# Decayed queries of each GLA head in a tile padded with zeros, in a hybrid GLA and HGRN2 decoder layer

## The chip, the cores and the metric

The kernel runs on one core of a Trainium2 chip. The metric is the device time of one execution in microseconds (us); smaller is better. Times are medians of several executions. A profile is one execution, recorded instruction by instruction. The engines are named as the profile names them: PE is TensorE (matmuls), PEld its loading of the stationary operand, DVE is VectorE, ACT is ScalarE, POOL is GpSimd, SP the engine that issues most DMAs.

## The reference

One decoder layer over 2048 tokens of width 1024, in float32: a mixer with two kinds of heads side by side (four GLA heads with 64 channels, four HGRN2 heads with 128 channels, all with values of width 128), an output projection, and an MLP with a squared ReLU. What the change touches is the gated linear attention of the heads:

```python
def step(S, inp):
    qi, ki, vi, bi = inp
    ...
    scores = jnp.einsum('bhid,bhjd,bhijd->bhij', qi, ki, decay)
    o = jnp.einsum('bhij,bhjv->bhiv', scores, vi) + jnp.einsum('bhid,bhdv->bhiv', qi * jnp.exp(bi), S)
    b_last = bi[:, :, -1:, :]
    S = S * jnp.exp(b_last)[:, :, 0, :, None] + jnp.einsum('bhjd,bhjv->bhdv', ki * jnp.exp(b_last - bi), vi)
    return S, o
```

Each chunk of tokens makes an output from two products: the masked scores with the values, and the decayed queries with the state carried so far.

## The kernel before

The tokens are worked in four blocks of 512, each of four chunks of 128 (the kernel's chunk is twice the reference's). In each block the mixer goes through four units in the order 0, 2, 3, 1. Units 0 and 1 hold two GLA heads each, units 2 and 3 two HGRN heads each. A unit first projects queries and keys with channels on the partitions (`zchan`), then values and gates with tokens on the partitions (`values`). These projections are the bulk of the work: each is three matmuls of 512 columns with operands split into a high and a low part (L301, L302, L303, "wide" in what follows).

The attention itself is a generator, `tile_task`, that is stepped between pieces of the projections. For a GLA unit the two heads share one tile: head 0 has its 64 channels on partitions 0 to 63, head 1 on 64 to 127. For HGRN a head fills the 128 partitions. The steps are:

- `decays`: cumulative sums of the log decays, three exponentials on ACT, then on DVE the products of keys and decay (L665) and of queries and decay (L666).
- `transposed` and `scores`: the keys are transposed on PE and copied by ACT (L723); the scores are made by L711 and L712, with 64 rows for a GLA head, and DVE writes them under the mask into a tile PT (L714, L715).
- `states`: one product of keys and values for each chunk (L735 for GLA, L738 for HGRN) and on DVE the running state of the four chunks in a tile St: L751 for the first, then L752 (add) and L754 (scale) for each further one. For GLA the two heads' states lie on the two halves of the partitions of one St.
- `outputs`: for each chunk, scores with values (L765) and queries with the state (L766), summed in one bank. L766 takes `q[rows, cols]` and `St[rows, cols]`, where `rows` is one half of the partitions for a GLA head and all 128 for HGRN.
- normalising, gating, a transpose back (L633), and the output projection.

All of this is full float32 (no split), and a product of this kind stands in the trace as two matmuls. The last unit's attention runs beside the output projection. DVE also does the second half of each sigmoid (L319, L547, L476) and the low parts of operands. The order on each engine is set ahead of time: instructions are placed by a scheduler that simulates the program with its own costs, so an edit at one place can move instructions of neighbouring tasks on every engine. Waits between engines are semaphores; each engine works through its own list in order.

`stage` gives [128, 1024] tiles from a pool of three (tag "st"). Before the change, two are only reserved at the start, and the pool is used from the end of the mixer on.

Of the kernel before, what the change touches and what calls it, by code (L numbers as in the profile page):

```python
# [16 lines left out]
P = 128  # L17
# [4 lines left out]
TB = 512  # L22
# [124 lines left out]
class Layer:  # L147
# [234 lines left out]
    def setup_mixer(self):  # L382
        nc = self.nc
        self.load_const("cmask")
        self.normw = self.static("norm_w", [P, 8])
        self.b_gk = self.static("b_gk", [P, 2])
        wgk = self.ct()[:16, :256]
        nc.sync.dma_start(wgk, self.io["w_gk_up"])
        self.wgk = self.split(self.small("wgk", (16, 256), F32R), self.small("wgk", (16, 256), F32R), wgk)
        lbr = self.static("hgrn_lower_bounds", [P, 4, 2])  # L390
        mx, den, self.lb, self.oml = (self.small(x, (P, 4)) for x in ("lbm", "lbd", "lb", "oml"))
        e = self.small("lbe", (P, 4, 2))
        nc.vector.tensor_max(mx, lbr[:, :, 0], lbr[:, :, 1])
        for r in range(2):
            nc.vector.tensor_sub(e[:, :, r], lbr[:, :, r], mx)
        nc.scalar.activation(e, e, AF.Exp)
        nc.vector.tensor_add(den, e[:, :, 0], e[:, :, 1])
        nc.vector.reciprocal(den, den)
        nc.vector.tensor_mul(self.lb, e[:, :, 0], den)
        nc.vector.tensor_scalar(self.oml, self.lb, -1.0, 1.0, ALU.mult, ALU.add)  # L400
        self.S, self.PT, self.npt = [], [], 0
        for i in range(6):
            self.S.append(self.small("S", (P, P)))
            nc.vector.memset(self.S[-1], 0.0)
        for i in range(2 if self.exact else 3):
            self.PT.append(self.small("PT", (P, TB)))
            nc.vector.memset(self.PT[-1], 0.0)
# [190 lines left out]
    def tile_task(self, u, i, q, k, g, scale):  # L598

        gla = u < 2  # L600
        heads = [(0, slice(0, 64)), (1, slice(64, P))] if gla else [(i, slice(0, P))]
        r, pts = yield from self.decays(q, k, g, scale)
        while self.vdone[u] < 3 and not self.exact:
            yield
        v, sg = self.vg[u]
        kT = self.transposed(k)
        if pts is None:
            pts = [self.next_pt() for _ in heads]
            mask = self.c["cmask"].unsqueeze(1).broadcast_to([P, NCH, P])
            for pt, (h, rows) in zip(pts, heads):  # L610
                self.scores(pt, q, k, rows, mask)
        yield
        while self.vdone[u] < 4:
            yield
        yield
        St = self.states(kT, r, v, gla, i, u if gla else 2 + 2 * (u - 2) + i)
        yield
        outs = []
        for pt, (h, rows) in zip(pts, heads):
            outs.append((h, *self.outputs(pt, q, St, v, h, rows)))  # L620
        yield
        for n, (h, o, rs) in enumerate(outs):
            og = self.ct()
            for j in range(NCH):
                cols = slice(j * P, (j + 1) * P)
                self.nc.vector.scalar_tensor_tensor(og[:, cols], o[:, cols], rs[:, j:j + 1],
                                                    sg[:, j, h * P:(h + 1) * P], ALU.mult, ALU.mult)
            outs[n] = (h, og)
        yield
        for h, og in outs:  # L630
            tr = self.at()
            for j in range(NCH):
                self.nc.tensor.transpose(tr[:, j * P:(j + 1) * P], og[:, j * P:(j + 1) * P], self.c["ident"])  # L633
            n = 2 * u + h
            self.oT[n] = self.split(*self.aslots(), tr, self.normw[:, n:n + 1])

    def decays(self, q, k, g, scale):

        nc, c = self.nc, self.c
        b = self.ct()  # L640
# [5 lines left out]
        r = self.t([P, 2, NCH], "r", bufs=6)  # L646
        if not self.exact:
            mid = b3[:, :, 63]
            d = g.rearrange("p (c t) -> p c t", t=P)
            nc.vector.tensor_sub(d, b3, b3[:, :, 63:64].broadcast_to([P, NCH, P]))  # L650
            nc.vector.tensor_scalar(g, g, LIMIT / scale, -LIMIT / scale, ALU.min, ALU.max)
            f = self.t([P, NCH], "fl", bufs=4)
            nc.vector.tensor_sub(r[:, 0, :], last, mid)
            flag = c["flag_a"] if scale != 1.0 else c["flag_b"]
            nc.vector.tensor_sub(f, b3[:, :, 0], mid)
            nc.vector.tensor_max(flag, flag, f)
            nc.vector.tensor_scalar_mul(f, r[:, 0, :], -1.0)
            nc.vector.tensor_max(flag, flag, f)
            nc.vector.tensor_copy(r[:, 1, :], mid)
            yield  # L660
            nc.scalar.activation(b, g, AF.Exp, scale=-scale)
            nc.scalar.activation(g, g, AF.Exp, scale=scale)
            nc.scalar.activation(r, r, AF.Exp, scale=scale)
            yield
            nc.vector.tensor_mul(k, k, b)  # L665
            nc.vector.tensor_mul(q, q, g)  # L666
            yield
            return r, None
        heads = (slice(0, 64), slice(64, P)) if scale != 1.0 else (slice(0, P),)
        pts = [self.next_pt() for _ in heads]  # L670
        for l, h in enumerate(LEVELS):
            mask = self.t([P, TB], "cti", I32, bufs=1)
# [22 lines left out]
        nc.scalar.activation(b, b, AF.Exp, scale=scale)  # L695
        nc.vector.tensor_mul(q, q, b)
        yield
        return r, pts

    def next_pt(self):  # L700
        self.npt += 1
# [851 lines left out]
```

## Time and profile before

| | |
|---|---|
| median of the timed runs | 2272.21 us (three runs, 2270.02 to 2276.08) |
| the profiled execution | 2269.14 us, span from first to last instruction 2267.3 us |
| granted TensorE clock | 0.995 |
| instructions in the span | 30672 |
| HBM read and written | 289.44 MB and 136.45 MB, 188 GB/s |

The mixer takes the first 960 us of the span; the MLP follows. In the profile a group of instructions has its line, engine, operation, output and input names, shape and count, then busy time in us and the mean of one in ns, then the idle time of the engine before it and what ended that. A timeline row has the start in us, the length drawn, engine, line, operation, names, shape and count. Matmuls are pipelined: the length drawn of one reaches over the start of the next, so the distance from start to start says what a matmul takes of the engine.

### The profile page before, as it was taken

How to read it: one execution, taken by the hardware profiler on the slowest of the kernel's cores; microseconds unless marked ns; L12 is line 12 of the kernel's file. 1: busy time of each engine (PE TensorE's matmuls, PEld its weight loads, DVE VectorE, ACT ScalarE, POOL GpSimd, SP SyncE). 2: the span in 40 equal slices, each digit the busy share in tenths (PEclk: the TensorE clock that was granted, in tenths of full speed). 3: DMA queues.
4: the chain of work that ended last, by engine and by line, in shares of the span. 5: the costliest groups of instructions: out<-in, count | busy, mean ns of one | idle time of the engine just before them, and what ended most of it. 6: DMA issues, size and time to landing. Idle time of an engine off the chain costs nothing.

```text
span 2267.3 us, 30672 instructions
## 1 busy us (share of the span) xinstructions
PE 2216.5 (98%) x10922; PEld 1830.8 (81%) x10922; DVE 1408.5 (62%) x2264; ACT 1089.3 (48%) x2104; POOL 643.5 (28%) x444
## 2 busy tenths in 40 slices
PE   8999999999999999999999999999999999999996
PEld 7788888888888978876888888888778878888884
DVE  6764565343652575377765686656536876777687
ACT  6764565334543554365555565555643322333255
POOL 4444301010100220035522343322322332232344
PEclk9999999999999999999999999999999999999998
DMA  7766974467545974378844474443434433443356
GB/s 244 262 232 241 322 257 149 138 237 281 181 151 176 349 286 158 130 270 281 294 151 152 177 238 163 152 153 144 176 126 135 130 123 110 130 140 117 116 148 132
DMA packets 249810, 428.02 MB, mean 189 GB/s; under 512 B 19872, under 2 KB 93872, under 8 KB 249648
## 3 DMA queue, kind: packets, MB, share of 16 engines
q1 hardware_dynamic: 245520, 418.10, 53.6%
q0 software_dynamic: 3552, 6.82, 1.9%
q8 instruction: 88, 1.44, 0.3%
q10 hardware_dynamic: 576, 1.05, 0.1%
q14 instruction: 74, 0.61, 0.1%
HBM read 289.44 MB, written 136.45 MB: 188 GB/s over the span
## 4 chain that ended last, share of the span: by engine, by line
PE 48%; DVE 2%; DMA 2%; ACT 2%; issue 1%; POOL 1%; SPq 0%; DVEq 0%; ACTq 0%; POOLq 0%
PE Y_f L1057 3%; PE Y_f L1059 3%; PE Y_f L1058 3%; PE Y_f L1358 3%; PE Y_f L1359 3%; PE Y_f L1360 3%; PE X_f L1358 2%; PE X_f L1360 2%; PE X_f L1359 2%; PE Z_f L1059 2%; PE Z_f L1057 2%; PE Z_f L1058 2%; PE Z_f L1360 2%; PE Z_f L1359 2%; PE Z_f L1358 2%; PE X_f L1059 2%
## 5 line engine op out<-in xcount | busy, mean ns | idle before, releaser
L301 PE MATMUL zp_f<-w_f,act_f 128*128 128x512 f32 (+2 forms) x896 | 328.6, 367 | 4.2 <-DVE ct_f L319 3.3
L302 PE MATMUL zp_f<-w_f,act_f 128*128 128x512 f32 (+2 forms) x896 | 325.0, 363 | 0.0
L303 PE MATMUL zp_f<-w_f,act_f 128*128 128x512 f32 (+2 forms) x896 | 323.4, 363 | 0.0
L944 ACT ACTIVATE u_f<-raw_f 128x1024 fp32r<-128x1024 f32 x107 | 113.6, 1061 | 331.9 <-PE Y_f L1359 225.4
L310 POOL TENSOR_TENSOR rs_f<-ms_f,c_neghalf 128x1 f32<-128x1 f32 (+1 forms) x80 | 65.1, 820 | 658.0 <-DVE ms_f L308 657.5
L938 POOL TENSOR_TENSOR u_f<-raw_f,u_f 128x1024 fp32r<-128x1024 f32 x49 | 120.4, 2457 | 305.5 <-ACT u_f L944 304.5
L301 PEld LDWEIGHTS zp_f<-w_f,act_f 128*128 128x128 f32 x896 | 168.6, 188 | 31.3 <-DVE ct_f L319 3.7
L303 PEld LDWEIGHTS zp_f<-w_f,act_f 128*128 128x128 f32 x896 | 168.7, 188 | 25.3 <-issue 0.5
L302 PEld LDWEIGHTS zp_f<-w_f,act_f 128*128 128x128 f32 x896 | 168.9, 189 | 24.3 <-issue 0.5
L301 PE MATMUL zp_f<-act_f,w_f 128*128 128x512 f32 x384 | 151.9, 399 | 7.9 <-ACT act_f L294 7.9
L302 PE MATMUL zp_f<-act_f,w_f 128*128 128x512 f32 x384 | 152.3, 397 | 0.1
L303 PE MATMUL zp_f<-act_f,w_f 128*128 128x512 f32 x384 | 151.9, 395 | 0.0
L1313 DVE TENSOR_TENSOR acc_f<-acc_f,Y_f 128x1024 f32<-128x1024 f32 (+1 forms) x91 | 107.5, 1182 | 64.5 <-PE Y_f L1360 63.2
L1358 PE MATMUL Y_f<-act_f,u_f 128*128 128x512 f32 x368 | 142.3, 390 | 4.8 <-ACT Y_f L1350 2.6
L1359 PE MATMUL Y_f<-act_f,u_f 128*128 128x512 f32 x368 | 143.4, 390 | 0.0
L1360 PE MATMUL Y_f<-act_f,u_f 128*128 128x512 f32 x368 | 142.8, 390 | 0.0
L292 POOL TENSOR_TENSOR w_f<-wr_f,w_f 128x512 fp32r<-128x512 f32 (+1 forms) x76 | 105.3, 1395 | 106.1 <-ACT w_f L291 105.4
L944 ACT ACTIVATE w_f<-t_f 128x512 fp32r<-128x512 f32 x128 | 80.1, 629 | 109.7 <-PE Y_f L1058 56.6
L1059 PE MATMUL X_f<-act_f,w_f 128*128 128x512 f32 x256 | 100.2, 391 | 3.6 <-DVE w_f L941 2.7
L1077 DVE TENSOR_TENSOR ev_f<-Y_f,p_f 128x512 f32<-128x512 f32 x94 | 64.6, 688 | 62.8 <-PE Y_f L1059 62.7
L1313 DVE TENSOR_TENSOR acc_f<-acc_f,Z_f 128x1024 f32<-128x1024 f32 (+1 forms) x62 | 73.2, 1181 | 47.6 <-PE Z_f L1360 47.4
L941 DVE TENSOR_TENSOR w_f<-t_f,w_f 128x512 fp32r<-128x512 f32 x96 | 79.9, 832 | 36.7 <-ACT w_f L944 36.7
(294 smaller groups left out, 5767.0 us busy)
## 6 DMA issues: line engine op xcount, KB each, us to landing
w_f<-w_split SPq DMA_DIRECT2D x188, 512.0 KB, 6.3
raw_f<-u_operands SPq DMA_DIRECT2D x224, 256.0 KB, 3.0
u_operands<-ev_f SPq DMA_DIRECT2D x223, 256.0 KB, 2.1
w_split<-w_f SPq DMA_DIRECT2D x64, 512.0 KB, 5.2
wr_f<-in_w_up SPq DMA_DIRECT2D x62, 512.0 KB, 3.5
wide_f<-in_x SPq DMA_DIRECT2D x32, 512.0 KB, 6.9
wr_f<-in_w_mix SPq DMA_DIRECT2D x64, 256.0 KB, 5.0
wr_f<-in_w_down SPq DMA_DIRECT2D x28, 512.0 KB, 4.8
```

The costliest lines, as they stand in the source:

```text
L301: mm(out, a[0], b[0], start=i == 0, stop=False)
L302: mm(out, a[0], b[1], start=False, stop=False)
L303: mm(out, a[1], b[0], start=False, stop=i == n - 1)
L938: nc.gpsimd.tensor_tensor(out, a, b, op)
L944: self.nc.scalar.activation(hi, raw, AF.Copy)
L1057: mm(z, whi[:, k, :], hi, start=first and k == 0, stop=False, skip_group_check=more)
L1058: mm(z, whi[:, k, :], lo, start=False, stop=False, skip_group_check=more)
L1059: mm(z, wlo[:, k, :], hi, start=False, stop=end, skip_group_check=more)
L1313: nc.vector.tensor_add(a[:, cols], a[:, cols], z[:, cols])
L1358: mm(zx, hi[:, k, tok], whi, start=not loaded and k == 0, stop=False, skip_group_check=loaded)
L1359: mm(zx, hi[:, k, tok], wlo, start=False, stop=False, skip_group_check=loaded)
L1360: mm(zx, lo[:, k, tok], whi, start=False, stop=k == 1, skip_group_check=loaded)
```

## The change

The decayed queries of a GLA tile are no longer written over the queries. A tile `self.queries` of [128, 1024] is made once and zeroed: its first 512 columns belong to head 0 of the unit, its last 512 to head 1. `decays` writes head 0's 64 rows of the product into the first half and head 1's 64 rows into the second; the rows of the other head's channels stay zero. `scores` still takes 64 rows, now from these tiles. `outputs` takes all 128 rows of a head's tile and of St, so that the other head's state is multiplied by zeros. The tile is shared by both GLA units and all blocks. HGRN heads and the exact variant (which is built but not run on this data) compute what they did.

```diff
@@ setup_mixer
+        if not self.exact:
+            x = self.stage()
+            nc.vector.memset(x, 0.0)
+            self.queries = [x[:, :TB], x[:, TB:]]
@@ tile_task
-        r, pts = yield from self.decays(q, k, g, scale)
+        r, pts, qs = yield from self.decays(q, k, g, scale)
...
-            for pt, (h, rows) in zip(pts, heads):
-                self.scores(pt, q, k, rows, mask)
+            for pt, qh, (h, rows) in zip(pts, qs, heads):
+                self.scores(pt, qh, k, rows, mask)
...
-        for pt, (h, rows) in zip(pts, heads):
-            outs.append((h, *self.outputs(pt, q, St, v, h, rows)))
+        for pt, qh, (h, rows) in zip(pts, qs, heads):
+            outs.append((h, *self.outputs(pt, qh, St, v, h, rows if self.exact else slice(0, P))))
@@ decays
             nc.vector.tensor_mul(k, k, b)
-            nc.vector.tensor_mul(q, q, g)
-            yield
-            return r, None
+            qs = self.queries if scale != 1.0 else [q]
+            for qh, rows in zip(qs, (slice(0, 64), slice(64, P)) if scale != 1.0 else (slice(0, P),)):
+                nc.vector.tensor_mul(qh[rows], q[rows], g[rows])
+            yield
+            return r, None, qs
```

Lines move by up to seven: L666 becomes L673, L754 becomes L761, L765 and L766 become L772 and L773. The order on SP stays the same, as does that of every engine after the mixer; PE, DVE, ACT and POOL change places within the mixer, mostly near the tiles of unit 0.

On VectorE, in the last block's unit 0, the product of queries and decay stands so before (ct_f are the [128, 512] working tiles; L476, L579, L596 belong to HGRN heads of unit 2):

```order
L643 SCALAR_TENSOR_TENSOR ct_f_7920<-c_ones,ct_f_7796 128x128 x4
L666 TENSOR_TENSOR ct_f_7238<-ct_f_7238,ct_f_7790 128x512
L596 TENSOR_TENSOR c_fmin<-c_fmin,fm_f_7894 128x1
L579 TENSOR_SCALAR ct_f_7797<-ct_f_7797 128x512
L476 TENSOR_TENSOR ct_f_7865<-zp_f_7803,ct_f_7865 128x512
L650 TENSOR_TENSOR ct_f_7796<-ct_f_7920 128x512
```

And so now (st_f_250 is the tile of padded queries):

```order
L648 SCALAR_TENSOR_TENSOR ct_f_7929<-c_ones,ct_f_7804 128x128 x4
L673 TENSOR_TENSOR st_f_250<-ct_f_7246,ct_f_7798 64x512
L600 TENSOR_TENSOR c_fmin<-c_fmin,fm_f_7902 128x1
L583 TENSOR_SCALAR ct_f_7805<-ct_f_7805 128x512
L673 TENSOR_TENSOR st_f_250<-ct_f_7246,ct_f_7798 64x512
L480 TENSOR_TENSOR ct_f_7873<-zp_f_7811,ct_f_7873 128x512
```

One instruction of 128 rows has become two of 64, with two HGRN steps between them.

A little later on VectorE, in the same tile, the state's updates (L752 and L754 on ct_f_8048) stand so among the HGRN steps before:

```order
L754 TENSOR_SCALAR ct_f_8048<-ct_f_8048,r_f_7855 128x128
L319 SCALAR_TENSOR_TENSOR ct_f_8011<-zp_f_7942,ct_f_8011 128x512
L651 TENSOR_SCALAR ct_f_7935<-ct_f_7935 128x512
L656 TENSOR_TENSOR c_flag_b<-c_flag_b,fl_f_8132 128x4
L752 TENSOR_TENSOR ct_f_8048<-ct_f_8048,at_f_8039 128x128
L657 TENSOR_SCALAR fl_f_8132<-r_f_8129 128x4
L754 TENSOR_SCALAR ct_f_8048<-ct_f_8048,r_f_7855 128x128
L658 TENSOR_TENSOR c_flag_b<-c_flag_b,fl_f_8132 128x4
L476 TENSOR_TENSOR ct_f_8011<-zp_f_7942,ct_f_8011 128x512
L752 TENSOR_TENSOR ct_f_8048<-ct_f_8048,at_f_8039 128x128
L665 TENSOR_TENSOR ct_f_7936<-ct_f_7936,ct_f_8124 128x512
L754 TENSOR_SCALAR ct_f_8048<-ct_f_8048,r_f_7855 128x128
```

And so now, from behind the first of the three scalings (L759 and L761 on ct_f_8057):

```order
L656 TENSOR_SCALAR ct_f_7944<-ct_f_7944 128x512
L319 SCALAR_TENSOR_TENSOR ct_f_8020<-zp_f_7951,ct_f_8020 128x512
L661 TENSOR_TENSOR c_flag_b<-c_flag_b,fl_f_8141 128x4
L759 TENSOR_TENSOR ct_f_8057<-ct_f_8057,at_f_8048 128x128
L662 TENSOR_SCALAR fl_f_8141<-r_f_8138 128x4
L670 TENSOR_TENSOR ct_f_7945<-ct_f_7945,ct_f_8133 128x512
L761 TENSOR_SCALAR ct_f_8057<-ct_f_8057,r_f_7863 128x128
L663 TENSOR_TENSOR c_flag_b<-c_flag_b,fl_f_8141 128x4
L480 TENSOR_TENSOR ct_f_8020<-zp_f_7951,ct_f_8020 128x512
L759 TENSOR_TENSOR ct_f_8057<-ct_f_8057,at_f_8048 128x128
L673 TENSOR_TENSOR ct_f_8020<-ct_f_8020,ct_f_7944 128x512
L761 TENSOR_SCALAR ct_f_8057<-ct_f_8057,r_f_7863 128x128
```

The key product of an HGRN head (L665, now L670) has moved ahead of the second scaling, and a query product of an HGRN head (L666, now L673), which stood behind the third scaling before, now stands ahead of it.

On TensorE, between the second and the third state products of that tile, before (at_f are output banks, zp_f_8139 a bank of a projection):

```order
L301 MATMUL zp_f_8139<-w_f_7729,act_f_7092 128x512
L302 MATMUL zp_f_8139<-w_f_7729,act_f_7092 128x512
L303 MATMUL zp_f_8139<-w_f_7729,act_f_7092 128x512
L766 MATMUL at_f_8086<-ct_f_8048,ct_f_7238 128x128
L765 MATMUL at_f_8086<-wide_f_7353,PT_f_264 128x128
L766 MATMUL at_f_8105<-ct_f_8048,ct_f_7238 128x128
L765 MATMUL at_f_8105<-wide_f_7353,PT_f_266 128x128
```

And now:

```order
L301 MATMUL zp_f_8148<-w_f_7737,act_f_7100 128x512
L302 MATMUL zp_f_8148<-w_f_7737,act_f_7100 128x512
L303 MATMUL zp_f_8148<-w_f_7737,act_f_7100 128x512
L301 MATMUL zp_f_8148<-w_f_7739,act_f_7121 128x512
L302 MATMUL zp_f_8148<-w_f_7739,act_f_7121 128x512
L303 MATMUL zp_f_8148<-w_f_7739,act_f_7121 128x512
L301 MATMUL zp_f_8148<-w_f_7741,act_f_7140 128x512
L302 MATMUL zp_f_8148<-w_f_7741,act_f_7140 128x512
L303 MATMUL zp_f_8148<-w_f_7741,act_f_7140 128x512
L301 MATMUL zp_f_8148<-w_f_7775,act_f_7161 128x512
L773 MATMUL at_f_8095<-ct_f_8057,st_f_250 128x128
L772 MATMUL at_f_8095<-wide_f_7361,PT_f_266 128x128
```

The third state product now has ten wide matmuls ahead of it where there were three.

More of the change, by code (lines that the diff above doesn't have):

```diff
@@ L697, in decays @@
         yield
-        return r, pts
+        return r, pts, [q] * len(heads)
     def next_pt(self):
```

## The prediction

> **What bounds the kernel now.** First I read the busy time of each engine on the page, then the same for the mixer alone (80 to 960 us, where all the changed work lies), then the list of waits of TensorE.
>
> ```profile
> PE 2216.5 (98%) x10922; PEld 1830.8 (81%) x10922; DVE 1408.5 (62%) x2264; ACT 1089.3 (48%) x2104; POOL 643.5 (28%) x444
> 80.00:960.00 880.00, 879.95 (x4988) 733.27 (x4988) 463.28 (x1200) 431.95 (x1088) 145.54 (x135) 1.00 0.63 220
> PE zp_f L301 <- ACT act_f L294: 7.9, 1, 7.9
> PE zp_f L301 <- DVE ct_f L319: 3.3, 1, 3.3
> ```
>
> In the second row the columns are the stretch, its length and the busy time of PE, PEld, DVE, ACT and POOL. PE is busy for 879.95 of 880 us, at a granted clock of 1.00. Of the waits the longest, 7.9 us, is the start, and the second row leaves 0.05 us for all that fall into its stretch. So in the mixer TensorE is the bound, and what counts there is how far apart its matmuls start, not how long each is drawn. VectorE is at 463 of 880 us, but it is not spread evenly, and that decides a part below.
>
> **The change, part by part.** *The state products.* The groups of L766, told apart by shape, show the 64-row ones (GLA) and the 128-row ones (HGRN) of the same line. Each product in full float32 stands as two matmuls ("pieces") in the trace, so 128 pieces are 64 products.
>
> ```profile
> L766 PE MATMUL at_f<-ct_f,ct_f 64*128 64x128 f32 x128 | 27.2, 323 | 0.0
> L766 PE MATMUL at_f<-ct_f,ct_f 128*128 128x128 f32 x128 | 22.4, 275 | 0.0
> ```
>
> By duration alone the two differ little (27.2 against 22.4 us). The start times say more. This is PE's timeline in the outputs of the last GLA tile (start, length drawn, line, shape, number):
>
> ```profile
> 952.25 0.39 PE L302 MATMUL zp_f<-w_f,act_f 128*128 128x512 f32 x1
> 952.57 0.49 PE L766 MATMUL at_f<-ct_f,ct_f 64*128 64x128 f32 x2
> 952.98 0.49 PE L765 MATMUL at_f<-wide_f,PT_f 128*128 128x128 f32 x2
> 953.40 0.49 PE L766 MATMUL at_f<-ct_f,ct_f 64*128 64x128 f32 x2
> 953.82 0.49 PE L765 MATMUL at_f<-wide_f,PT_f 128*128 128x128 f32 x2
> 954.24 0.49 PE L766 MATMUL at_f<-ct_f,ct_f 64*128 64x128 f32 x4
> 954.66 0.49 PE L765 MATMUL at_f<-wide_f,PT_f 128*128 128x128 f32 x2
> 955.08 0.48 PE L766 MATMUL at_f<-ct_f,ct_f 64*128 64x128 f32 x2
> 955.49 0.49 PE L765 MATMUL at_f<-wide_f,PT_f 128*128 128x128 f32 x2
> 955.91 0.49 PE L766 MATMUL at_f<-ct_f,ct_f 64*128 64x128 f32 x2
> 956.32 0.50 PE L303 MATMUL zp_f<-w_f,act_f 128*128 128x512 f32 x1
> 956.66 0.39 PE L301 MATMUL zp_f<-w_f,act_f 128*128 128x512 f32 x1
> ```
>
> And this is the same code for an HGRN head, where both lines have 128 rows:
>
> ```profile
> 122.90 0.39 PE L301 MATMUL zp_f<-act_f,w_f 128*128 128x512 f32 x1
> 123.13 0.38 PE L765 MATMUL at_f<-wide_f,PT_f 128*128 128x128 f32 x2
> 123.35 0.39 PE L766 MATMUL at_f<-ct_f,ct_f 128*128 128x128 f32 x2
> 123.58 0.39 PE L765 MATMUL at_f<-wide_f,PT_f 128*128 128x128 f32 x2
> 123.80 0.39 PE L766 MATMUL at_f<-ct_f,ct_f 128*128 128x128 f32 x2
> 124.02 0.39 PE L765 MATMUL at_f<-wide_f,PT_f 128*128 128x128 f32 x2
> 124.17 0.48 PE L302 MATMUL zp_f<-act_f,w_f 128*128 128x512 f32 x1
> 124.48 0.39 PE L303 MATMUL zp_f<-act_f,w_f 128*128 128x512 f32 x1
> ```
>
> A wide matmul (L301 to L303, 512 columns) takes 0.23 us from start to start (122.90 to 123.13). The HGRN stretch, 122.90 to 124.48, holds two wide ones and five products: (1.58 - 0.46) / 5 = 0.224 us for a product. The GLA stretch, 952.25 to 956.66, holds two wide ones and ten products (six of L766, four of L765): (4.41 - 0.46) / 10 = 0.395 us. The L765 between them are slow too (0.42 us from 952.98 to 953.40), though their shape is that of HGRN: it is the going over between 64 and 128 rows that costs, on both sides of each group of 64-row pieces. With 128 rows the ten would take 2.24 us, so this stretch gives 1.71 us for its six products, 0.285 each.
>
> A tile of unit 0 is laid out a little differently. Its outputs in the last block, first L765 to the wide one behind the last L766:
>
> ```profile
> 820.52:829.87 9.35, 9.35 (x48) 6.56 (x47) 9.29 (x26) 4.29 (x10) 2.62 (x2) 1.00 0.62 240
> 87.55 0.49 PE L766 MATMUL at_f<-ct_f,ct_f 64*128 64x128 f32 x2
> ```
>
> Two of the 48 began before; of the other 46, 14 are wide and 32 are the pieces of 8 L765 and 8 L766. (9.35 - 14 x 0.23) / 16 = 0.383 us; at 0.224 the 16 take 3.58 instead of 6.13 us: 2.55 us for the tile, 0.32 for each L766. From 87.55 to 955.91 us I count 56 such groups of 64-row pieces, seven in each of eight tiles. So the four tiles of unit 0 give 4 x 2.55 = 10.2 us, the four of unit 1 give 4 x (1.71 + 2 x 0.32) = 9.4 us: 19.6 us in all. After the change none of the 56 is left; the scores (L711, L712) and L735 keep their small shapes and their price.
>
> One rule speaks against this. On "TensorE: Matmul & The Clock Gate", section "Part 3: Packing small matmuls — row/col tiling", the Trainium skill says that matmuls on different row groups of the array run beside each other, some 4 ns apart. By it two 64-row products of two heads cost what one does, and zeros throw that away; by the rows above only the x4 at 954.24 has it (0.42 us for two products), one group in seven, and I keep the 19.6 us.
>
> *What VectorE gets more.* The product of queries and decay becomes two of 64 partitions by 512.
>
> ```profile
> L666 DVE TENSOR_TENSOR ct_f<-ct_f,ct_f 128x512 f32<-128x512 f32 x24 | 17.0, 707 | 1.1 <-ACT ct_f L662 1.1
> L714 DVE COPY_PREDICATED PT_f<-c_cmask,at_f 64x512 f32<-64x512 int32 x32 | 23.3, 727 | 37.6 <-PE at_f L712 37.6
> L407 DVE MEMSET PT_f<- 128x512 f32 x3 | 1.5, 485 | 0.2
> ```
>
> No row shows a 64x512 product. It lies between half of 707 ns (nothing is added) and 707 ns (one whole product is added); I take the upper end, since the nearest row with 64 partitions of 512 (L714, 727 ns) is no shorter than one with 128: 0.7 us in each of eight tiles, 5.6 us in all. It lies beside the wide matmuls of a busy PE and costs nothing where VectorE has time to spare; without that cover it is the 5.6 us. The zeroing (128x1024, about 2 x 0.485 = 1 us) lies at the start, where TensorE waits 7.9 us for an ACT result anyway: 0, or 1 us if that cover were gone. The tile is the third of its pool; its next taker comes after the mixer, and a whole unit lies between two uses of it, so new waits for its release cost 0.
>
> *What is late next.* In the unit-0 tile of the last block VectorE is busy for 9.29 of 9.35 us. There the state that L766 reads is ready only just in time. L754 writes it:
>
> ```profile
> 823.35 0.34 DVE L754 TENSOR_SCALAR ct_f<-ct_f,r_f 128x128 f32<-128x128 f32 x1
> 824.12 0.48 PE L766 MATMUL at_f<-ct_f,ct_f 64*128 64x128 f32 x2
> 825.90 0.34 DVE L754 TENSOR_SCALAR ct_f<-ct_f,r_f 128x128 f32<-128x128 f32 x1
> 826.49 0.48 PE L766 MATMUL at_f<-ct_f,ct_f 64*128 64x128 f32 x2
> 828.72 0.33 DVE L754 TENSOR_SCALAR ct_f<-ct_f,r_f 128x128 f32<-128x128 f32 x1
> 829.11 0.49 PE L766 MATMUL at_f<-ct_f,ct_f 64*128 64x128 f32 x4
> ```
>
> The three have 0.43, 0.25 and 0.06 us to spare. Take the last: TensorE would be there 6 x 0.32 = 1.9 us sooner by the six products before it; the new order puts seven more wide matmuls before it (1.6 us later); VectorE reaches L754 0.7 us later by the added product and another 0.7 us later because the new order puts one HGRN product more before it. 0.06 - 1.9 + 1.6 - 1.4 = -1.6 us: TensorE waits 1.6 us of this tile's 2.55. Behind the waiting L766 stand only matmuls, which lose the same. The first tile is nearly as crowded (third figure of engine time in this row, VectorE, 18.88 of 20 us):
>
> ```profile
> 80.00:100.00 20.00, 19.95 (x131) 14.91 (x130) 18.88 (x52) 12.84 (x29) 2.83 (x3) 1.00 0.75 259
> ```
>
> I charge it with 0.5 us, nearer to nothing than to the 1.6 of the last block, since its state products have more wide matmuls between them. Together 2.1 us; bounds are 0 and the whole 10.2 us of the unit-0 tiles.
>
> **Sum.** 19.6 - 2.1 = 17.5 us less. The rows come from an execution of 2269.14 us (span 2267.3), which becomes 2251.6. That execution lies 3.07 us under the median of the timed runs, 2272.21 (2270.02 to 2276.08), so the forecast for the median is 2254.7 us, 0.77% faster. After 960 us the order of instructions is the same on every engine; the stage behind moves up as it is.
>
> **The rivals.** (1) *VectorE becomes the bound* in all four unit-0 tiles, not in one: their 10.2 us go, and the added product, 4 x 0.7 = 2.8 us, shows. Gain 19.6 - 10.2 - 2.8 = 6.6 us, 2265.6 us. For it: 9.29 of 9.35 us. Against it: in the sum above even the most crowded tile keeps a third of its gain. (2) *Only durations count*: the slow starts beside the 64-row pieces have another reason (the order, the full-float32 L765), and 27.2 - 22.4 = 4.8 us is all: 2267.4 us. Against it: HGRN runs the same two lines in the same alternation at 0.224. (3) *Lost overlap, the slower side*: zeros double the rows that are run for nothing. If the two heads' 64-row products had all run beside each other, 64 products cost 32 x 0.224 = 7.2 us before and 64 x 0.224 = 14.3 us now: 7.2 us more, 2279.4 us (+0.3%). It decides only if such pairs are the rule and the going over is free; the rows show one pair in seven groups. That the change does not do what it says is not open: all 64 products have 128 rows in the new order.
>
> **How the numbers follow.** The forecast has 0.84, with a range of its own from 2250 to 2261; (1) has 0.08, (2) 0.04, (3) 0.04. The low end, 2249, takes 64 x 0.32 = 20.5 us, no new wait, and the lowest of the runs shown (2.2 us under their median). The high end, 2264, takes half the unit-0 gain away (19.6 - 2.1 - 5.1 = 12.4 us) and the scatter upward (3.9 us); it leaves out (1), (2) and (3), 0.16. A measurement of this kernel can tell about 0.3% from no change, 6.8 us. So faster holds the forecast, 0.84; within 0.3% are (1) and (2), 0.12; slower is (3), 0.04.
>
> **What would show it.** Right, if the line that was L766 has one shape, 128*128, if ten products of a GLA stretch take about 2.2 us and the L765 between them 0.22 us each, and if TensorE now has waits of about 1.6 us in all for the state update (L754) near 810 us. The product of queries should stand as 64x512 at 0.7 us, twice in each tile. Wrong, if the L765 beside the state products stay at 0.42 us (2), if waits for VectorE add up to 10 us in the four unit-0 tiles (1), or if TensorE gains what I say and a new wait after 960 us takes it back.

## The result and the profile after

The changed kernel takes 2256.22 us, the median of six runs (2252.61 to 2258.14); the kernel before took 2272.32 us beside it (2269.99 to 2276.08, six runs). The ratio is 0.9929, with a 95% interval of 0.9919 to 0.9939: 16.1 us faster, with an interval of 13.9 to 18.4 us. The forecast was 2254.7 us, in a range from 2249 to 2264.

The profiled execution of the changed kernel took 2258.14 us (span 2256.3), the longest of its six, and that of before 2269.14 us, shorter than any of the six runs above. So the two traces differ by 11.0 us and the medians by 16.1; the runs of the two kernels once more, below, show where this difference lies.

Lines from 600 on have moved down by up to seven: L766 is now L773, L765 is L772, L754 is L761, L666 is L673, L715 is L722. First the busy times of the page, then the groups of PE between 80 and 945 us, told apart by shape, that answer to those of before:

```profile
PE 2201.9 (98%) x10922; PEld 1830.0 (81%) x10922; DVE 1416.8 (63%) x2273; ACT 1090.1 (48%) x2104; POOL 643.5 (29%) x444
```

```profile
L772 PE MATMUL at_f<-wide_f,PT_f 128*128 128x128 f32 x256 | 46.7, 275 | 1.2 <-DVE PT_f L722 1.2
L773 PE MATMUL at_f<-ct_f,st_f 128*128 128x128 f32 x128 | 24.0, 279 | 2.5 <-DVE ct_f L761 2.5
L773 PE MATMUL at_f<-ct_f,ct_f 128*128 128x128 f32 x128 | 22.5, 275 | 0.4 <-DVE ct_f L761 0.4
```

The products with the state have one shape; those of GLA are the ones that read `st_f`, the padded tiles. Behind the second bar stands idle time of PE before them, which was 0.0 for the state products of before: 2.9 us for the state update L761 (2.5 of them before GLA products, 0.4 before an HGRN product), 1.2 us for the masked scores L722. PE's timeline in the outputs of the last GLA tile, the place that the prediction shows of before:

```profile
940.09 0.39 PE L302 MATMUL zp_f<-w_f,act_f 128*128 128x512 f32 x1
940.32 0.38 PE L773 MATMUL at_f<-ct_f,st_f 128*128 128x128 f32 x2
940.54 0.39 PE L772 MATMUL at_f<-wide_f,PT_f 128*128 128x128 f32 x2
940.76 0.39 PE L773 MATMUL at_f<-ct_f,st_f 128*128 128x128 f32 x2
...
942.10 0.39 PE L772 MATMUL at_f<-wide_f,PT_f 128*128 128x128 f32 x2
942.32 0.39 PE L773 MATMUL at_f<-ct_f,st_f 128*128 128x128 f32 x2
942.47 0.48 PE L303 MATMUL zp_f<-w_f,act_f 128*128 128x512 f32 x1
942.78 0.40 PE L301 MATMUL zp_f<-w_f,act_f 128*128 128x512 f32 x1
```

From 940.09 to 942.78 it is 2.69 us where it was 4.41; less two wide matmuls (0.46) the ten products take 0.223 us each, as HGRN's did. The L772 beside them start 0.22 us apart, not 0.42, with no change to them.

To follow the time through the program, take the same wide matmul (by its place in PE's list) in two traces and compare its start. L303 behind this tile stood at 956.32 us before and stands at 942.47 now: 13.85 us earlier. The table does this by stretches of the mixer, bounded by wide matmuls that start at 80.5, 230.1, 812.3, 906.9 and 994.1 us in the first trace of before. Each number is what the stretch gained against that trace, in us; the last two columns are the sum at the end of the mixer (here the last L303, at 994.1 us before, behind the output projection) and at the last wide matmul of the program. The other rows are the experiments that follow.

| kernel | start | block 1: both GLA tiles | blocks 2, 3: four tiles | block 4: unit 0 | block 4: unit 1 | mixer | program |
|---|---|---|---|---|---|---|---|
| changed | -0.7 | 3.1 | 9.7 | -0.5 | 2.3 | 13.9 | 10.9 |
| changed, once more | -0.3 | 2.9 | 9.5 | -0.5 | 2.3 | 13.8 | 9.7 |
| before, once more | 0.0 | 0.0 | -0.4 | -1.0 | 0.0 | -1.4 | -4.5 |
| e1, split only | 0.0 | -1.3 | -0.4 | -2.6 | 0.0 | -4.3 | -6.4 |
| e2, rows only | -0.4 | 4.3 | 9.7 | -0.2 | 2.3 | 15.7 | 13.4 |
| e3, pairs | 0.1 | 3.3 | 5.6 | 0.3 | 1.3 | 10.6 | 8.5 |
| e4, scores of 128 rows | -0.2 | 3.4 | 8.2 | -1.2 | 2.0 | 12.1 | 8.5 |
| e5, half product on GpSimd | -1.4 | 4.0 | 9.5 | -0.7 | 2.3 | 13.7 | 12.0 |
| e6, copies on ScalarE | -0.4 | 4.7 | 9.7 | 0.5 | 2.3 | 16.7 | 17.7 |
| e7, sums later | -0.2 | 3.7 | 9.7 | 2.0 | 2.3 | 17.6 | 17.8 |
| e8, both | 0.2 | 4.5 | 9.7 | 2.5 | 2.3 | 19.1 | 16.7 |
| e9, no sums | -0.3 | 3.8 | 9.7 | 2.5 | 2.3 | 18.1 | 17.8 |

Six of the eight tiles gained what the forecast gave them (2.33 us in unit 1, 2.5 in unit 0). The first unit-0 tile and the last did not. The first, measured alone (wide matmuls at 80.5 and 106.2 us before), gained 1.4 us, and block 4's lost 0.5. Block 1 lost another 0.7 us at an HGRN tile, between 121 and 130 us. In the first unit-0 tile the timeline of the changed kernel, VectorE and GpSimd together and then PE's wait, shows where the missing microsecond comes from:

```profile
77.70 1.29 POOL L292 TENSOR_TENSOR w_f<-wr_f,w_f 128x512 fp32r<-128x512 f32 x1 [3.58 <-ACT w_f L291]
78.22 3.03 DVE L673 TENSOR_TENSOR st_f<-ct_f,ct_f 64x512 f32<-64x512 f32 x2
79.27 1.44 POOL L292 TENSOR_TENSOR w_f<-wr_f,w_f 128x512 fp32r<-128x512 f32 x1 [0.27 <-ACT w_f L291]
...
88.96 0.46 PE L772 MATMUL at_f<-wide_f,PT_f 128*128 128x128 f32 x2 [1.19 <-DVE PT_f L722]
```

The two half products of this tile take 1.32 and 1.68 us (3.03 together) where the other fourteen take 0.66 to 0.69, and each ends 0.54 us behind a GpSimd product of the weights (L292). Before, the one undivided product met one of these:

```profile
77.79 1.32 DVE L666 TENSOR_TENSOR ct_f<-ct_f,ct_f 128x512 f32<-128x512 f32 x1
```

### The profile page after: what moved, and what is told of

Its sections match the earlier page's. It is cut to its first block, busy times and chain, and to the rows that moved or that the text cites. A ratio compares the mean times of both kernels' runs of the same rounds, so it can differ in the third digit from the quotient of the medians.

```text
span 2256.3 us, 30683 instructions
## 1 busy us (share of the span) xinstructions
PE 2201.9 (98%) x10922; PEld 1830.0 (81%) x10922; DVE 1416.8 (63%) x2273; ACT 1090.1 (48%) x2104; POOL 643.5 (29%) x444
## 4 chain that ended last, share of the span: by engine, by line
PE 49%; DMA 2%; DVE 1%; ACT 1%; issue 1%; POOL 1%; SPq 0%; DVEq 0%; ACTq 0%; POOLq 0%
PE Y_f L1365 4%; PE Y_f L1366 3%; PE Y_f L1367 3%; PE Y_f L1064 3%; PE Y_f L1065 3%; PE Y_f L1066 3%; PE X_f L1365 2%; PE X_f L1367 2%; PE Z_f L1064 2%; PE Z_f L1065 2%; PE X_f L1366 2%; PE Z_f L1066 2%; PE Z_f L1365 2%; PE Z_f L1367 2%; PE X_f L1066 2%; PE Z_f L1366 2%
## 5 line engine op out<-in xcount | busy, mean ns | idle before, releaser
L303 PE MATMUL zp_f<-w_f,act_f 128*128 128x512 f32 (+2 forms) x896 | 323.1, 363 | 0.0
L303 PEld LDWEIGHTS zp_f<-w_f,act_f 128*128 128x128 f32 x896 | 168.8, 188 | 24.6 <-issue 0.5
L303 PE MATMUL zp_f<-act_f,w_f 128*128 128x512 f32 x384 | 151.9, 396 | 0.0
L292 POOL TENSOR_TENSOR w_f<-wr_f,w_f 128x512 fp32r<-128x512 f32 (+1 forms) x76 | 104.5, 1385 | 102.3 <-ACT w_f L291 98.4
```

Source lines behind the costliest of these rows:

```text
L303: mm(out, a[1], b[0], start=False, stop=i == n - 1)
```

## The experiments

Theory at the start: 128 rows and the crossings that go give 19.6 us, and what is missing of it was taken by waits on VectorE, which has one half product more in each tile. Rivals: the new order of instructions makes the gain; only durations count; the loss in the two tiles has nothing to do with the half product. Each experiment was timed in turns with the kernel before on the same chip (2271.44 us for e1 to e4, 2271.9 for e5 to e8).

### e1: the split alone

```diff
-            outs.append((h, *self.outputs(pt, qh, St, v, h, rows if self.exact else slice(0, P))))
+            outs.append((h, *self.outputs(pt, qh, St, v, h, rows)))
```

> The changed kernel, but the products with the state go back to 64 rows (rows of the head's own tile and of the state); the zeroed tiles, the two half products on VectorE and the new order stay. Theory (the gain is the 128 rows at 0.224 us a product and the crossings that go; VectorE's extra half product only costs waits): the time of the kernel before or up to 4 us more, 2272 to 2276 us, with the mixer's end at 996 us or later. Rival (the gain comes from the order or from the tiles being apart, not from the rows): as the changed kernel, about 2256 us.

Measured: 2274.41 us (2271.92 to 2275.93), ratio 1.0013 (1.0004 to 1.0021). The order is that of the changed kernel, the time is not: the whole gain comes with the 128 rows. The price of the split and of the order that came with it shows in the table: 1.3 us in block 1 (1.0 of them in the first tile, where PE waits 1.18 us for L722), 2.6 us in block 4's unit 0 and next to nothing elsewhere. In block 4 it is there as a wait for the state update, which takes 1.29 us beside a GpSimd sum (PE's timeline of e1):

```profile
830.84 0.48 PE L773 MATMUL at_f<-ct_f,st_f 64*128 64x128 f32 x2 [0.99 <-DVE ct_f L761]
```

### e2: the rows alone

```diff
-            outs.append((h, *self.outputs(pt, q, St, v, h, rows)))
+            outs.append((h, *self.outputs(pt, q, St, v, h, rows if self.exact else slice(0, P))))
```

> The kernel before, but each product with the state takes all 128 rows of the undivided queries and of the state; both heads' states are thus added into both heads' outputs, so the output is another one. No split on VectorE, no zeroing, the order of before. Theory: the whole of the forecast's gain from rows and crossings, 19.6 us, less 1 to 2 us in the unit-0 tile of the last block: 2252 to 2255 us, 2 to 4 us faster than the changed kernel, with 2.3 to 2.5 us in the two unit-0 tiles (first and last block) that gained 0.5 and -0.5 us in the changed kernel. Rival (only the durations count): at most 4.8 us faster than before, 2267 us. Rival (what the first and last unit-0 tiles lost has nothing to do with VectorE's extra half product): as the changed kernel, 2256 us.

Measured: 2255.04 us (2252.83 to 2258.55), ratio 0.9929 (0.9916 to 0.9942). By time it can't be told from the changed kernel, and the 2 to 4 us that were expected are not shown; by the trace its mixer ends 1.8 us sooner. "Only durations count" falls: 19.6 us were forecast from crossings, and 15.7 are there without any other edit. In block 1 the theory holds (4.3 of 4.9 us; the wait for the masked scores is 0.24 us here, 1.19 in the changed kernel). In block 4 it misses: there is no half product here, and the unit-0 tile still gained nothing (-0.2). All of e2's timeline around one wait, engines together, in order of time:

```profile
809.82 1.36 DVE L754 TENSOR_SCALAR ct_f<-ct_f,r_f 128x128 f32<-128x128 f32 x1
809.84 1.26 POOL L919 TENSOR_TENSOR wide_f<-wide_f 128x512 f32<-128x512 f32 x1 [13.51 <-DMA h_operands<-wide_f]
811.10 0.68 DVE L319 SCALAR_TENSOR_TENSOR ct_f<-zp_f,ct_f 128x512 f32<-128x512 f32 x1
...
811.23 0.38 PE L766 MATMUL at_f<-ct_f,ct_f 128*128 128x128 f32 x1 [1.34 <-DVE ct_f L754]
```

The state update takes 1.36 us where it takes 0.34 elsewhere, and it ends 0.08 us behind a sum on GpSimd (L919). The changed kernel has the same picture:

```profile
811.50 1.26 POOL L926 TENSOR_TENSOR wide_f<-wide_f 128x512 f32<-128x512 f32 x1 [13.69 <-DMA h_operands<-wide_f]
811.52 1.32 DVE L761 TENSOR_SCALAR ct_f<-ct_f,r_f 128x128 f32<-128x128 f32 x1
...
812.89 0.49 PE L773 MATMUL at_f<-ct_f,st_f 128*128 128x128 f32 x2 [1.59 <-DVE ct_f L761]
```

These sums belong to `combine`, which prepares the operands of the second stage's first product beside the last block. In the second trace of the changed kernel (r1 below) the first update is not held, but the second takes 1.28 us, and PE waits 0.66 and then 1.78 us: as much in all. That gave a second theory: VectorE's instructions are held while GpSimd's run, and in that tile this, more than the half product, makes PE wait.

### e3: 64 rows in pairs, no zeros

```diff
+        for j in range(NCH):
+            cols = slice(j * P, (j + 1) * P)
+            for o, pt, (h, rows) in zip(os, pts, heads):
+                nc.tensor.matmul(o[:, cols], pt[:, cols], v[:, j, h * P:(h + 1) * P], start=True, stop=False)
+            for o, pt, (h, rows) in zip(os, pts, heads):
+                nc.tensor.matmul(o[:, cols], q[rows, cols], St[rows, cols], start=False, stop=True)
```

> The kernel before with 64-row products, no zeros and no split, but the two heads' outputs of a GLA tile are made chunk by chunk together, so that the 64-row products of the two heads (rows 0 to 63 and 64 to 127) stand next to each other, and the 128-row ones too. Tests whether 64-row pairs overlap and what a crossing costs. Theory (a crossing costs, and pairs of other rows overlap): four products of 1.58 us alternating cost about 1.06 us in pairs, so that the 8 tiles win 10 to 16 us: 2256 to 2262 us. Rival (64-row products cost their 0.2 us each wherever they stand): within 3 us of before, 2269 to 2275 us.

Measured: 2264.07 us (2260.03 to 2267.73), ratio 0.9968 (0.9957 to 0.9979): 2 us slower than the theory's range, and out of the rival's as well. The mixer of its trace, with 10.6 us, lies at the lower end of the 10 to 16 us that were expected. PE's timeline in the last GLA tile of e3, where the two heads' products now stand in fours:

```profile
942.34 0.39 PE L302 MATMUL zp_f<-w_f,act_f 128*128 128x512 f32 x1
942.65 0.49 PE L784 MATMUL at_f<-ct_f,ct_f 64*128 64x128 f32 x4
943.08 0.71 PE L782 MATMUL at_f<-wide_f,PT_f 128*128 128x128 f32 x4
943.72 0.49 PE L784 MATMUL at_f<-ct_f,ct_f 64*128 64x128 f32 x4
944.14 0.71 PE L782 MATMUL at_f<-wide_f,PT_f 128*128 128x128 f32 x4
944.78 0.49 PE L784 MATMUL at_f<-ct_f,ct_f 64*128 64x128 f32 x4
945.20 0.50 PE L303 MATMUL zp_f<-w_f,act_f 128*128 128x512 f32 x1
```

Four 64-row matmuls of two heads go by in 0.43 us (942.65 to 943.08), no longer than two of one head did before (0.41 from 952.57 to 952.98). So they do run beside each other, which is what the Trainium skill states on "TensorE: Matmul & The Clock Gate", section "Part 3: Packing small matmuls — row/col tiling". Four products come to 1.07 us, as estimated (1.06), and a unit-1 tile gains 1.8 us. Not every pair forms: in unit-0 tiles the scheduler still places one chunk's products one by one, so that of the 56 groups of 64-row products 36 are left (32 if every pair stood together); the unit-0 tiles of blocks 2 and 3 gained 1.2 us each. And even in its best place the pair loses: 1.07 us for four products against 4 x 0.223 = 0.89 us over 128 rows, since each group still has a crossing on both sides.

### e4: zeros in the scores too

```diff
-                self.scores(pt, qh, k, rows, mask)
+                self.scores(pt, qh, k, slice(0, P), mask)
```

> The changed kernel, but the GLA scores too go over 128 rows of the head's zero-padded queries and of the undivided keys (same sums), so that the two heads' 64 by 64 score products can no longer stand beside each other in the array. In the changed kernel the two heads' scores of a tile take 1.52 us (83.09 to 84.61) as 64-row products, against about 1.05 us for one head of 128 rows (157.14 to 158.2). Theory (crossings cost, but here rows 0 to 63 and 64 to 127 overlap, which zeros give up): 2 x 1.05 less 1.52 = 0.5 us more in each of 8 tiles, less a crossing of 0.2 us: 2 to 4 us slower than the changed kernel, 2258 to 2260 us. Rival (128 rows are better wherever 64 stood): 1 to 3 us faster, 2253 to 2255 us.

Measured: 2257.42 us (2256.5 to 2261.82), ratio 0.9942 (0.9929 to 0.9955). The mixer ends 1.7 us later than in the changed kernel's two traces; a unit-1 tile loses 0.36 us (2.33 to 1.97). The medians, 1.2 us apart, can't tell the two kernels apart; in the trace the sign is that of the theory, the size a little less. The two heads' scores stand side by side in one long group, and the theory's reading is that zeros take overlap away there and save one crossing in a tile only. "128 rows are better wherever 64 stood" falls.

### e5: half the product on GpSimd

```diff
-                nc.vector.tensor_mul(qh[rows], q[rows], g[rows])
+                (nc.gpsimd if rows.start == 64 else nc.vector).tensor_mul(qh[rows], q[rows], g[rows])
```

> The changed kernel, but the second head's half product of a GLA tile (64 by 512) runs on GpSimd instead of VectorE. In the changed kernel's trace VectorE instructions on SBUF tiles that meet a GpSimd product are held until it ends (a 128x128 update 1.32 us instead of 0.34 while GpSimd ran 1.26). Theory (the two engines exclude each other, so GpSimd's 1.3 us holds VectorE longer than the 0.69 us it saves): 0 to 3 us slower than the changed kernel, 2256 to 2259 us, with VectorE instructions beside the half products drawn 1 us longer. Rival (only VectorE's own work counts, and GpSimd has room): 1 to 3 us faster, 2253 to 2255 us.

Measured: 2257.46 us (2256.18 to 2261.72), ratio 0.9948 (0.9933 to 0.9962); the mixer ends 13.7 us before that of before, as in the changed kernel. As a whole, taking half the work off VectorE won nothing: the first tile gained 2.5 us instead of 1.4, with no wait for L722, and 0.7 us more was lost at the start, where PE's granted clock was 0.50 for 6.8 us from 74 us on (3.4 us in the changed kernel). Whether the edit or chance lengthened that stretch stays open. The groups of the half product, in e5 and then in the changed kernel, both from 80 us on:

```profile
L673 POOL TENSOR_TENSOR st_f<-ct_f,ct_f 64x512 f32<-64x512 f32 x7 | 10.9, 1561 | 69.7 <-DVE fm_f L599 49.0 <-ACT ct_f L667 20.5 <-POOL wide_f L915 0.2
L673 DVE TENSOR_TENSOR st_f<-ct_f,ct_f 64x512 f32<-64x512 f32 x7 | 6.9, 984 | 0.0
```

```profile
L673 DVE TENSOR_TENSOR st_f<-ct_f,ct_f 64x512 f32<-64x512 f32 x15 | 11.2, 745 | 0.2
```

VectorE's own half is drawn 0.24 us longer on average (984 against 745 ns): in two tiles it takes 1.79 us beside GpSimd's, the microsecond that was expected, in the others 0.66 to 0.85. GpSimd needs 1.56 us for its half.

### e6 to e8: without the half product, without the sums in that tile, and both

In e6 VectorE makes the undivided product of before, the scores use 64 rows of it, and ScalarE copies the halves into the padded tiles:

```diff
                 self.scores(pt, qh, k, rows, mask)
+            if gla:
+                qs = self.queries
+                for qh, (h, rows) in zip(qs, heads):
+                    self.nc.scalar.activation(qh[rows], q[rows], AF.Copy)
```

In e7 the task with the sums starts behind unit 0 of the last block:

```diff
-                self.spawn(self.combine(0, halves))
             for u in UNITS:
+                if u == UNITS[1] and b == NBLK - 1:
+                    self.spawn(self.combine(0, halves))
```

e8 has both edits. (In e6 `decays` is as before the change.)

> The changed kernel, but VectorE makes the undivided product of before, the scores take 64 rows of that, and ScalarE copies the two halves into the zeroed tiles behind the scores; the products with the state have 128 rows. Same results. Theory (the extra half product of VectorE cost the first block's unit-0 tile 1.3 to 1.5 us and the last block's 0.3 us): the mixer ends 15 to 16 us before that of the kernel before (13.9 in the changed kernel), so 2253.5 to 2255.5 us, with no product with the state waiting for ScalarE. Rival (ScalarE's copies come late and take the place of VectorE's wait): as the changed kernel or slower, 2256 to 2259 us, with waits of PE on the copies.

> The changed kernel, but the sums for the first product of the second stage (16 GpSimd sums of 128x512 with their loads and stores) start behind unit 0 of the last block instead of before it. Same results. Theory (in the last block's unit-0 tile VectorE is the bound, held by these GpSimd sums for 1 to 1.3 us at a time, once the rows give PE its 2.5 us back): the tile gains 2.3 to 2.6 us as those of the second and third block instead of -0.5, the mixer ends 16.5 to 17.5 us before that of before, 2252 to 2254 us, 2 to 4 us faster than the changed kernel. Rival (the tile's loss comes from the extra half product alone): the tile stays under +0.5 us and the time at 2255 to 2257 us.

> Both of the two: ScalarE copies instead of the split product, and the sums behind unit 0 of the last block. Theory: the two gains add up, since they lie in different tiles, to the forecast's full 19.6 us less about 0.5: the mixer ends 18 to 19.5 us before that of before, 2250.5 to 2253 us. Rival (what is won in the mixer is given back by a later wait at the start of the second stage): 2253 to 2256 us with a mixer that ends 18 us earlier.

Measured: e6 2252.95 us (2251.07 to 2256.5), ratio 0.9929 (0.9915 to 0.9943); e7 2252.36 us (2250.81 to 2255.66), ratio 0.9923 (0.9909 to 0.9937); e8 2253.21 us (2251.27 to 2254.07), ratio 0.9921 (0.9907 to 0.9934). In the traces the mixer ends 16.7, 17.6 and 19.1 us sooner than that of before, and block 4's unit-0 tile gains 0.5, 2.0 and 2.5 us. e8 does what was expected; e6 gains 0.7 us more than its range, and e7's tile 0.3 us less. The windows from 80 to 900 us of the changed kernel and of e8 (busy time of PE, PEld, DVE, ACT, POOL) show where it was:

```profile
80.00:900.00 820.00, 815.94 (x4729) 690.97 (x4728) 451.36 (x1149) 414.72 (x1029) 142.38 (x131) 1.00 0.65 228
```

```profile
80.00:900.00 820.00, 819.87 (x4753) 695.12 (x4752) 440.03 (x1149) 424.52 (x1058) 141.99 (x132) 1.00 0.65 229
```

PE's 4.06 us without work (the 2.9 and 1.2 us of waits above) are 0.13 us in e8. ScalarE's copies, 16 of 631 ns, cost nothing that the trace shows:

```profile
L619 ACT ACTIVATE st_f<-ct_f 64x512 f32<-64x512 f32 x16 | 10.1, 631 | 4.2 <-DVE ct_f L675 4.1
```

So the mixer of e8 has the forecast's 19.6 us but for half a microsecond. (In e6 and e8 VectorE's undivided product of the first tile takes 1.32 us, as before the change, and PE does not wait for the scores there.) By the medians all three lie about 3 us below the changed kernel, but their ratios overlap with its own: they are faster in the mixer, by 2.9 to 5.2 us in the traces, and that they are faster as a whole is likely and not shown. The rival of e8 has some truth: of its 19.1 us 2.4 were gone at the end of the second stage. The two traces that follow show what this is worth.

### The two kernels once more

> The changed kernel once more, for the scatter of one program and beside its own runs of before. By the theory the first stage repeats to about 0.1 us behind the first 100 us (the mixer ends 13.9 us before that of before), and what differs from the earlier profile lies in the second stage, in steps of 1 to 2 us at its loads; time 2253 to 2258 us. Rival: the tiles' gains themselves differ from run to run by a microsecond.

> The kernel before once more, one profile. By the theory its first stage lies within 0.3 us of the earlier profile at every tile, and its second stage up to 4 us later, as its median of 2272 us against the 2269.1 us of the earlier profiled run suggests. Rival: the first stage scatters as much as the second.

Measured: the changed kernel 2256.57 us (2254.29 to 2259.44), ratio 0.9933 (0.992 to 0.9947), against 2270.88 us for before; the single run of before 2273.36 us. The changed kernel's mixer repeats to 0.1 us at its end and to 0.3 us in each stretch behind the start. Two experiments widen this: e7 and e9 have the changed kernel's instructions in the same order up to 724 us, and there block 1 gained 3.7 and 3.8 us instead of 3.1 and 2.9. The first unit-0 tile gained the same 1.4 us in all four; the difference is the HGRN tile, where in the two traces of the changed kernel an update L761 met a GpSimd product (1.32 us from 124.94 us on, in the first) and PE waited 0.41 and 0.34 us, and in e7 and e9 lost nothing. The mixer of before doesn't repeat either: its unit-0 tile of block 4 lost 1.0 us, by the same hold (second trace of before, all engines):

```profile
823.84 1.36 DVE L754 TENSOR_SCALAR ct_f<-ct_f,r_f 128x128 f32<-128x128 f32 x1
823.84 1.28 POOL L919 TENSOR_TENSOR wide_f<-wide_f 128x512 f32<-128x512 f32 x1 [12.88 <-DMA h_operands<-wide_f]
...
825.25 0.48 PE L766 MATMUL at_f<-ct_f,ct_f 64*128 64x128 f32 x2 [0.63 <-DVE ct_f L754]
```

In the first trace of before GpSimd's sum began at another moment and met an instruction that nobody waited for:

```profile
824.04 1.27 POOL L919 TENSOR_TENSOR wide_f<-wide_f 128x512 f32<-128x512 f32 x1 [14.18 <-DMA h_operands<-wide_f]
824.21 1.39 DVE L651 TENSOR_SCALAR ct_f<-ct_f 128x512 f32<-128x512 f32 x1
```

One program in one order, with and without the hold on an update that PE needs: this is the plainest sign that the hold makes the wait. And behind the mixer the second trace of before lost 3.1 us on the first (4.5 less 1.4), as much as most of the other kernels did (1.8 to 4.1 us). The first trace of before was a lucky one, then, and the "losses" behind the mixer need not be an answer to the change: by the same measure e6 gained 1.0 us there and before lost 3.1 on itself. Nor is there a new wait: PE's idle time behind the mixer is 24.6 us in the first trace of before and 24.0 in that of the changed kernel. What differs is the granted clock. In the changed kernel's trace it is 0.50 for 3.4 us four times there (from 1031, 1062, 1625 and 2209 us), which costs up to 1.7 us each (half of 3.4), in the first trace of before once, in its second twice, in e9 once. What sets these stretches was not looked into.

### e9: which part of the sums' task holds the tile

```diff
-            nc.gpsimd.tensor_add(a22, a21, a22)
+            s and nc.gpsimd.tensor_add(a22, a21, a22)
```

and likewise for the other three kinds of sum (`s` is 0 for these).

> The changed kernel without the 16 GpSimd sums for the first product of the second stage; their loads, ScalarE scalings and stores stay where they were, so that the operands stored are the scaled inputs and not their sums. It tells apart what of these sums' work held the unit-0 tile of the last block. Theory (GpSimd's instructions hold VectorE's): the tile gains 2.0 to 2.6 us on before, as when the whole task is moved (2.0 and 2.5), against -0.5 in the changed kernel, and no 128x128 update of the state lasts over 0.5 us there. Rival (ScalarE's scalings or the transfers of that task hold it): the tile stays within 0.6 us of -0.5. One profile; the time of one run may lie anywhere from 2250 to 2257 us.

Measured: 2250.95 us in its one run. The tile gained 2.5 us, with loads, ScalarE scalings and stores where they were. The group of the state update on VectorE, from 795 to 850 us, in e9 and in the changed kernel:

```profile
L761 DVE TENSOR_SCALAR ct_f<-ct_f,r_f 128x128 f32<-128x128 f32 x9 | 2.8, 341 | 0.0
```

```profile
L761 DVE TENSOR_SCALAR ct_f<-ct_f,r_f 128x128 f32<-128x128 f32 x9 | 3.8, 449 | 0.0
```

No update is held any more, and the half product is still there. So GpSimd's sums are what makes this tile late. (With the sums gone some neighbouring instructions also change places; the two traces of before, which share one order, show the hold without that.)

## Why the prediction was right, and where it was off

**The bound.** Right: PE's starts set the time of the mixer. Where the products with the state became cheaper and nothing made PE wait, the whole saving reached the next wide matmul, to 0.1 us a tile.

**The price of a crossing.** Right in mechanism and size. Forecast 2.35 us for a tile of unit 1 and 2.55 for one of unit 0; measured 2.33 and 2.5. e1 shows that it is the rows, e2 that the rows do it alone, e3 that it is the crossing: even where pairs overlap, four products cost 1.07 us against 0.89. The sum of 19.6 us is reached in e8 (19.1).

**VectorE's extra work.** Forecast: 0.7 us for a product of 64 partitions, hidden. Measured: 0.66 to 0.69 us in fourteen of sixteen, and 1.32 and 1.68 us in the first tile, beside GpSimd; hidden in six tiles of eight (e1: 0.4 us in all of blocks 2 and 3, as much as the two traces of before differ there).

**The new waits.** This is the term that was mis-sized. Charged: 0.5 us for the first unit-0 tile and 1.6 for the last, 2.1 in all. Measured: 1.1 and 3.1, 4.2 in all, and 0.7 us more at an HGRN tile that was charged with nothing; with 0.7 us at the start this is what lies between 19.6 and the 13.9 us of the mixer. PE's waits on L722 and L761 are 4.1 of it. The step that failed is the one that took VectorE's instructions as long as most of them are drawn in the trace of before and moved them as they were ("0.06 - 1.9 + 1.6 - 1.4", with the half product at 0.7 us and L754 at 0.34). All three losses show VectorE instructions held beside GpSimd: the half products of the first tile, 3.0 us instead of 1.4, and the updates L761, 1.32 us instead of 0.34. So the wait came at other products than forecast, too. The sum was made for the last of the tile's three state updates and put 1.6 us there; PE waited 1.59 us for the first and 0.87 for the second (0.66 and 1.78 in the second trace) and not at all for the third. That 1.59 is close to 1.6 is chance. The sign that this could happen stood in the trace of before, as VectorE instructions of both tiles drawn a microsecond too long (L651 with 1.39 us, L666 with 1.32), and was not followed up. In the first tile the wait for L722 is 1.0 to 1.2 us in every trace with both half products on VectorE and at most 0.24 in those without (e2, e3, e5, e6, e8), so there it goes with the split.

**The order behind 960 us.** "The stage behind moves up as it is" holds for the order, and no new wait took the gain back. In time this stage varies by up to 5 us from one trace to the next, more than the missed term.

**The shift to the median.** The forecast took the profiled execution of before as 3.07 us under its median and shifted the sum by it. That came out right by luck, for a reason it didn't know: this trace escaped the hold in block 4 and was quick behind the mixer. The 16.1 us between the medians are 13.9 us of the mixer's gain against that lucky trace and 15.2 (13.8 + 1.4) against the second; the rest is within the runs' scatter. So the 16.1 us come closer to the forecast's 17.5 than its sum deserves: trace against trace the mixer gained 13.9.

**The rivals.** (1), VectorE as the bound in all four unit-0 tiles, falls: two of them gained 2.5 us, and waits for VectorE add up to 4.1 us in the mixer, not to 10. (2), only durations, falls with e2. (3), the lost overlap, is real where 64-row products stand together (e3, and e4 with 0.36 us a tile) and loses to the crossings where they alternate with 128 rows.

## What to carry to other kernels

A small matmul in a stream of full ones is not to be priced by its length: compare the starts of the same line with and without it, and count the changes of shape. Zeros that make all shapes alike are cheap in such a stream and cost overlap in a block of small products that stand together. Before an edit speeds up PE beside a crowded VectorE, look for instructions of VectorE that are drawn longer than their group's usual length, find what ran on GpSimd at that moment, and ask what else could be caught there; here moving a GpSimd task that wasn't urgent and handing a copy to ScalarE together gave back what the waits had cost in the mixer (19.1 of 19.6 us).

## What the hardware showed that was not expected

In these traces VectorE instructions are held while a GpSimd instruction runs, and whether they are goes with where their operands lie. Matching start and end times in the changed kernel's trace: of the state updates L761, which read only SBUF tiles, 12 of 72 ran beside a GpSimd instruction and took 0.77 us on average, the other 60 took 0.34. Of the products L630, which read a PSUM tile, 77 of 128 ran beside one, and both kinds took 0.34 us. The same shows within one operation, the TENSOR_TENSOR: L759, which reads one PSUM tile, took 0.28 us either way (8 of 96 beside GpSimd), L670, which reads only SBUF tiles, up to 1.39 us beside one (797 us) and 0.69 otherwise. The Trainium skill states on "SBUF — State Buffer", section "SBUF: two separate sides", that the two engines share a port pair as an exclusive lock for a whole instruction; the rows here agree (1.32 us beside 1.26).

The second thing is how exact the rest is: of two runs of one program, the stretch from 230 to 812 us of the changed kernel differs by 0.2 us, while the stage behind 994 us differs by 1.1 us there and by 3.1 us for the kernel before. In the first stage a gain of a microsecond can be read from one trace each at a tile where no instruction was held; where one was, two traces of the same program differed by up to 1.0 us. From the times it can't be read.
